# A hybrid diffusion layer on one core: retention moved beside the last recurrent pair, the output projection in one piece

## The chip, the core and the metric

The kernel runs on one core of a Trainium2 chip. The metric is the device time of one execution in microseconds (us). Five engines run their own instruction streams in order and meet at semaphores: TensorE (PE, matrix products; its weight loads are listed as PEld), VectorE (DVE), ScalarE (ACT), GpSimd (POOL), and SyncE (SP), which here issues every DMA from one queue. A profile is one execution recorded by the hardware.

## What is computed

One layer (depth 1, batch 1) over 512 latent tokens of width 2048, with 256 context tokens as a prefix. The part of the reference that the change touches:

```python
p = xm @ w_in                                         # xm: normalised, modulated latent tokens
o_rw, _ = rwkv_group(dwconv_seq(p[..., :RW_COLS], rw_conv), s_rw_c, *rw_params, readout=True)
o_ret, _ = retention_group(p[..., RW_COLS:], s_ret_c, rope=True, readout=True)
out = jnp.concatenate([o_rw, o_ret], axis=-1) @ w_out
...
x = x + g1 * rmsnorm(out, norm_post_mix[l])
h = rmsnorm(x, norm_pre_ffn[l]) * (1.0 + sc2) + sh2
y = conv_ffn(h, ffn_w_gate[l], ffn_w_up[l], ffn_conv[l], ffn_conv_b[l], ffn_w_down[l], rows)
x = x + g2 * rmsnorm(y, norm_post_ffn[l])
```

`rwkv_group` is a recurrence over 16 heads of 64 columns, `retention_group` is attention with a fixed decay over 8 heads of 128 columns. Both write 1024 of the 2048 columns that `w_out` reads. The modulation vectors (`g1`, `sh2`, `sc2`, `g2`; the kernel calls them `mod` 0 to 3) are products of one vector with a 2048 x 2048 matrix each.

## The kernel before

The code names instructions for each engine in Python; a scheduler then orders them by data, free buffers and the order in which they were named, and fixes one order per engine ahead of time. An engine that waits holds up everything behind it in its order, and so does the DMA queue on SP.

**Dense products.** Each weight block is fetched (`raw`), split into a high and a low part (`whi` on ACT, `wlo` on DVE), and each of the 16 slices of 128 rows takes three products of 128x128 by 128x512 on PE. The input projection of one 128-column tile has 16 such slices (L541 to L543).

**The recurrence.** Heads go in eight pairs. For a pair there are a preparation, a triangular solve (30 serial steps on DVE, L1182 and L1183, then small products on PE, L1197 and L1206) and a chain of eight steps (`rw_chain`: L1263, L1270, L1277, L1237, L1291 on PE with copies on ACT, sums on DVE, and one copy per direction on POOL), after which `rw_out` (PE lines L428, L441, L1335 to L1338) stores the pair's 128 rows into `o_mix` in HBM (L1340). Period p runs the chain of pair p and the preparation and solve of pair p+1, with a list `TILES` saying how many projection tiles are named among them. `behind` lets a solve's first product stand behind the projection products named so far.

**Modulation.** `ada_rest` computes one `mod` vector with 64 DVE steps of 128x512 (L846, L848) on blocks `adaw` that come by DMA, and four groups of tiny PE products (L852). `mod` 1 is spread over the periods, one step per 20 units of projection (`ADA`).

**Retention.** After the last pair, `ret_phase` fetches `o_mix` back (tile `om`), splits it into `hh` and `hl`, and runs the eight heads in two streams (even and odd heads, the second two units later), with the first half of the output projection (`out_steps`, 128 slices, L730 to L732) and all of `mod` 0 merged in by weight. A head (`retention`) loads v (`rv`), q and k (`rx`), their rotated halves (`rxs`, four DMAs each), decay tables (`dec`, `gam`), the state (`rst`) and the gate (`rg`); it turns v on PE (L767), rotates q and k (DVE L773 and L776, POOL L775), scales q twice on POOL (`qd`, L782), forms four score blocks (PE L787) that DVE multiplies by the decay (`prob`, L789), sums them (PE L800) and adds the state's part (PE L804), normalises on ACT and DVE (L808 to L812), turns the result back (PE L816) and gates it (`ro`, DVE L818). `mix_out` then runs the second half of the output projection, adds the halves and takes the norms; the ConvGLU part follows.

## Time and profile before

| | |
|---|---|
| median of 3 runs | 3353.15 us (3351.7 to 3360.01) |
| profiled execution | 3356.21 us, of which the span from first to last instruction is 3354.3 us |
| PE busy | 3168.1 us, 94% of the span |
| DVE busy | 2081.7 us, 62% |
| ACT busy | 1120.0 us, 33% |
| POOL busy | 237.5 us, 7% |
| mean granted PE clock | 0.968 of full speed |

The shares are means over stages that differ. Below, a stretch is named by its time from the span's start; a granted clock of 1.0 is 2.4 GHz and 0.5 is 1.2 GHz. "Idle before" is time in which an engine stood still just ahead of an instruction, with the instruction or transfer that ended it.

### The profile page before, as it was taken

How to read it: one execution, taken by the hardware profiler on the slowest of the kernel's cores; microseconds unless marked ns; L12 is line 12 of the kernel's file. 1: busy time of each engine (PE TensorE's matmuls, PEld its weight loads, DVE VectorE, ACT ScalarE, POOL GpSimd, SP SyncE). 2: the span in 40 equal slices, each digit the busy share in tenths (PEclk: the TensorE clock that was granted, in tenths of full speed). 3: DMA queues.
4: the chain of work that ended last, by engine and by line, in shares of the span. 5: the costliest groups of instructions: out<-in, count | busy, mean ns of one | idle time of the engine just before them, and what ended most of it. 6: DMA issues, size and time to landing. Idle time of an engine off the chain costs nothing.

```text
span 3354.3 us, 50276 instructions
## 1 busy us (share of the span) xinstructions
PE 3168.1 (94%) x19672; PEld 2507.3 (75%) x19672; DVE 2081.7 (62%) x3562; ACT 1120.0 (33%) x1954; POOL 237.5 (7%) x381
## 2 busy tenths in 40 slices
PE   5999999999999999997999899999999999999997
PEld 3688888766666776765777688888888888788885
DVE  4474767787877877765677856335643555345544
ACT  3333245434344344432232433223222222223322
POOL 0000011001111111111210100000000000000001
PEclk9999999999999999997999899999999999999998
DMA  8732222542243422426768433332423333333242
GB/s 286 272 104 77 78 84 91 157 122 89 92 148 100 150 89 88 128 69 217 232 227 280 152 110 127 110 102 94 145 90 99 101 97 104 119 104 98 95 143 102
DMA packets 197724, 433.64 MB, mean 129 GB/s; under 512 B 25360, under 2 KB 49680, under 8 KB 197488
## 3 DMA queue, kind: packets, MB, share of 16 engines
q1 hardware_dynamic: 197488, 430.45, 39.9%
q8 instruction: 154, 2.52, 0.3%
q14 instruction: 82, 0.67, 0.1%
HBM read 399.75 MB, written 30.61 MB: 128 GB/s over the span
## 4 chain that ended last, share of the span: by engine, by line
PE 47%; issue 3%; DMA 3%; DVE 2%; POOL 1%; ACT 0%; SPq 0%; POOLq 0%; DVEq 0%; ACTq 0%
PE gbank L179 14%; PE gbank L181 14%; PE gbank L180 14%; DMA adaw<-ada 2%; DVE adacc L848 1%; PE bank L787 0%; POOL y L909 0%; PE obank L732 0%; PE obank L731 0%; PE obank L730 0%; DVE wlo L204 0%; PE gbank L897 0%; PE bank L852 0%; PE gbank L898 0%; PE gbank L899 0%
## 5 line engine op out<-in xcount | busy, mean ns | idle before, releaser
L161 DVE TENSOR_TENSOR wlo<-raw,whi 128x1024 fp32r<-128x1024 f32 (+1 forms) x336 | 342.3, 1019 | 618.1 <-ACT whi L160 609.2
L160 ACT CAST whi<-raw 128x1024 fp32r<-128x1024 f32 (+1 forms) x336 | 297.1, 888 | 898.9 <-PE gbank L180 869.5
L179 PE MATMUL gbank<-hh,whi 128*128 128x512 f32 x1376 | 535.6, 389 | 0.0
L181 PE MATMUL gbank<-hh,wlo 128*128 128x512 f32 x1376 | 535.4, 389 | 0.0
L180 PE MATMUL gbank<-hl,whi 128*128 128x512 f32 x1376 | 535.4, 389 | 0.0
L203 ACT CAST whi<-raw 128x512 fp32r<-128x512 f32 (+2 forms) x320 | 211.0, 660 | 512.6 <-PE gbank L542 241.3
L543 PE MATMUL gbank<-xh,wlo 128*128 128x512 f32 (+1 forms) x896 | 367.8, 411 | 6.2 <-DVE wlo L204 6.1
L542 PE MATMUL gbank<-xl,whi 128*128 128x512 f32 (+1 forms) x896 | 368.9, 412 | 0.0
L541 PE MATMUL gbank<-xh,whi 128*128 128x512 f32 (+1 forms) x896 | 368.2, 411 | 0.2
L204 DVE TENSOR_TENSOR wlo<-raw,whi 128x512 fp32r<-128x512 f32 (+2 forms) x320 | 237.5, 745 | 102.4 <-ACT whi L203 97.5
L181 PEld LDWEIGHTS gbank<-hh,wlo 128*128 128x128 f32 x1376 | 258.3, 188 | 53.8
L180 PEld LDWEIGHTS gbank<-hl,whi 128*128 128x128 f32 x1376 | 258.3, 188 | 53.5
L179 PEld LDWEIGHTS gbank<-hh,whi 128*128 128x128 f32 x1376 | 258.3, 188 | 53.5
L181 PE MATMUL gbank<-dh,wlo 128*128 128x512 f32 x704 | 278.1, 395 | 0.2
L179 PE MATMUL gbank<-dh,whi 128*128 128x512 f32 x704 | 278.1, 395 | 0.0
L180 PE MATMUL gbank<-dl,whi 128*128 128x512 f32 x704 | 277.8, 395 | 0.0
L938 DVE SCALAR_TENSOR_TENSOR cacc<-grid,fprm,cacc 128x512 f32<-128x512 f32 x352 | 264.2, 751 | 9.9 <-ACT cacc L935 1.3
L848 DVE SCALAR_TENSOR_TENSOR adacc<-adaw,sc,adacc 128x512 f32<-128x512 f32 x240 | 187.0, 779 | 79.3 <-DMA adaw<-ada 78.0
L543 PEld LDWEIGHTS gbank<-xh,wlo 128*128 128x128 f32 (+1 forms) x896 | 170.2, 190 | 49.8 <-DVE wlo L204 8.8
L541 PEld LDWEIGHTS gbank<-xh,whi 128*128 128x128 f32 (+1 forms) x896 | 170.5, 190 | 41.4 <-issue 4.7
L542 PEld LDWEIGHTS gbank<-xl,whi 128*128 128x128 f32 (+1 forms) x896 | 170.4, 190 | 38.3 <-issue 3.1
L181 PEld LDWEIGHTS gbank<-dh,wlo 128*128 128x128 f32 x704 | 132.3, 188 | 33.4 <-DVE wlo L161 1.0
(305 smaller groups left out, 4984.1 us busy)
## 6 DMA issues: line engine op xcount, KB each, us to landing
raw<-w_in SPq DMA_DIRECT2D x284, 256.0 KB, 3.0
adaw<-ada SPq DMA_DIRECT2D x192, 256.0 KB, 3.3
raw<-w_gate SPq DMA_DIRECT2D x88, 512.0 KB, 3.7
raw<-w_up_ffn SPq DMA_DIRECT2D x88, 512.0 KB, 3.6
ada<-ada SPq DMA_DIRECT2D x64, 512.0 KB, 6.1
raw<-w_down SPq DMA_DIRECT2D x64, 512.0 KB, 3.5
raw<-w_out SPq DMA_DIRECT2D x32, 512.0 KB, 5.0
adaw<-ada SPq DMA_DIRECT2D x32, 512.0 KB, 4.5
```

What stands on the lines that cost most here:

```text
L160: nc.scalar.copy(hi[:, 0:n, 0:m], raw[:, 0:n, 0:m])
L161: nc.vector.tensor_tensor(lo[:, 0:n, 0:m], raw[:, 0:n, 0:m], hi[:, 0:n, 0:m].bitcast(F32), op=ALU.subtract)
L179: self.nc.tensor.matmul(o, hi, xh(k), start=(k == 0), stop=False)
L180: self.nc.tensor.matmul(o, hi, xl(k), start=False, stop=False)
L181: self.nc.tensor.matmul(o, lo, xh(k), start=False, stop=(k == nk - 1))
L203: nc.scalar.copy(hi[:, 0:n, 0:m], raw[:, 0:n, 0:m])
L204: nc.vector.tensor_tensor(lo[:, 0:n, 0:m], raw[:, 0:n, 0:m], hi[:, 0:n, 0:m].bitcast(F32), op=ALU.subtract)
L541: self.nc.tensor.matmul(o, hi, xh[k], start=(k == 0), stop=False)
L542: self.nc.tensor.matmul(o, hi, xl[k], start=False, stop=False)
L543: self.done = self.nc.tensor.matmul(o, lo, xh[k], start=False, stop=(k == KT - 1))
L848: nc.vector.scalar_tensor_tensor(acc, w[:, k], c, acc, op0=ALU.mult, op1=ALU.add)
L938: nc.vector.scalar_tensor_tensor(acc, grid[:, dy:dy + 8, dx:dx + 64], cw[:, f, i:i + 1], acc, op0=ALU.mult, op1=ALU.add)
```

## The change

Four things move. The list `TILES` names all 62 projection tiles within the first seven latent periods, so that none is left for the last pair. `mod` 0 follows `mod` 1 in the same periods, one step per 10 units instead of 20. The eight retention heads run in the last pair's chain: the two streams of heads and the chain with its `rw_out` are merged with equal weight and with no projection among them; the heads' pools take the place of the latent input tiles, with three instead of four buffers for `rx` and `rxs`, the decay table in a work tile, and the PSUM banks of the recurrence. A head's result is no longer split on the spot but stored into `o_mix`, now with 16 rows of tiles. The whole output projection (256 slices) then stands in `mix_out`, behind 16 loads of `om` through three buffers and their splits, with `mod` 2 spread over it at 2 and 3 steps per column tile in place of 3.

```diff
-TILES = [4, 5, 3, 5, 4, 4, 4, 5, 5, 6, 5, 5, 4]
+TILES = [4, 5, 3, 5, 4, 4, 5, 5, 6, 6, 5, 5, 5]
...
-ADAW = 3
-ADA = 20
+ADAW = 2
+ADA = 10
...
-        ada = self.ada_rest(ap, 1, 1, 2)
+        ada = chain(self.ada_rest(ap, 1, 1, 2), self.ada_rest(ap, 0, 1, 2))
...
-        for p in range(NP):
-            todo = take(len(tiles) if p == NP - 1 else TILES[nc_ + 2 + p])
-            B, steps = period(B, p)
-            fill(todo, (steps, 1.0))
+        for p in range(NP - 1):
+            work = chain(self.rw_chain(B), self.rw_out(B))
+            B = self.latent(p + 1)
+            steps = merge((work, chain_time(False), EARLY),
+                          (chain(self.rw_prep(B), self.rw_fill(B)), prep + fill_time(False), 1.0), lead=True)
+            fill(take(TILES[nc_ + 2 + p]), (steps, 1.0))
+        fill(tiles)
         pull(ada)
         esa.close()
+        esl.close()
+
+        with ExitStack() as esr:
+            self.rp = self.pool(esr, "ret", side="right", reuse_waits="tile")
+            self.rope = self.rp.tile([128, 2, L], F32, name="rope")
+            self.nc.sync.dma_start(self.rope, self.a["rope"])
+            heads = [self.retention(h) for h in range(NH)]
+            drain(merge((chain(self.rw_chain(B), self.rw_out(B)), chain_time(False), 1.0),
+                        (chain.from_iterable(heads[0::2]), 44, 1.0), (chain([LAG], chain.from_iterable(heads[1::2])), 44 + LAG, 1.0)))
...
-    def ret_phase(self):
-
...
-        drain(back())
-        heads = [self.retention(h) for h in range(NH)]
-        ada = self.ada_rest(self.rp, 0, 1, 2)
-        drain(merge((chain.from_iterable(heads[0::2]), 44, 1.0), (chain([LAG], chain.from_iterable(heads[1::2])), 44 + LAG, 1.0),
-                    (out(), OUT[0] + OUT[1], 1.0), (ada, KT // 4 * KT, ADAR)))
...
-            x = ld(i, "rx", 4)
-            xs = tile("rxs", bufs=4)
+            x = ld(i, "rx", 3)
+            xs = tile("rxs", bufs=3)
...
-            t = tile("rtmp", bufs=1)
-            nc.gpsimd.tensor_tensor(t, xs, self.rope[:, 1], op=ALU.mult)
-            nc.vector.tensor_tensor(y, y, t, op=ALU.add)
+            nc.gpsimd.tensor_tensor(xs, xs, self.rope[:, 1], op=ALU.mult)
+            nc.vector.tensor_tensor(y, y, xs, op=ALU.add)
...
-        self.split(o, self.hh[NP + h], self.hl[NP + h])
+        nc.sync.dma_start(self.o_mix[NP + h], o)
...
     def mix_out(self):
         nc, a, mp = self.nc, self.a, self.mp
+        order = [*range(NP, KT), *range(NP)]
+        ys = [self.yp.tile([128, L], F32, name=f"y{c}") for c in range(KT)]
+        for k in order:
+            t = mp.tile([128, L], F32, name="om", bufs=3)
+            nc.sync.dma_start(t, self.o_mix[k])
+            self.split(t, self.hh[k], self.hl[k])
+        wst = self.stream([a["w_out"][c, :, k:k + 8] for c in range(KT) for k in (NP, 0)])
         acc = mp.tile([128, L], F32, name="acc")
-        ys = self.ys
         ada = self.ada_rest(mp, 2)
         for c in range(KT):
             ps = self.gbank()
-            drain(self.out_steps(ps, 1))
-            nc.vector.tensor_tensor(ys[c], ps, ys[c], op=ALU.add)
-            sq = self.square(mp, ys[c])
+            for k in order:
+                hi, lo = next(wst)
+                nc.tensor.matmul(ps, hi, self.hh[k], start=(k == NP), stop=False)
+                nc.tensor.matmul(ps, hi, self.hl[k], start=False, stop=False)
+                nc.tensor.matmul(ps, lo, self.hh[k], start=False, stop=(k == NP - 1))
+            sq = self.square(mp, ps)
+            nc.scalar.copy(ys[c], ps)
...
-            pull(ada, ADAW)
+            pull(ada, ADAW + c % 2)
```

What this makes of the engines' orders shows at three places. The line numbers of the changed program differ from those above, and the names say which operation it is.

**SP, the loads of the third and fourth head.** Before, they stand among the blocks of `mod` 0 (`adaw`):

```order
L743 DMA rv<-ret_t 128x512
L832 DMA adaw<-ada 128x512
L743 DMA rx<-ret_t 128x512
L755 DMA rxs<-ret_t 32x512
L832 DMA adaw<-ada 128x512
L755 DMA rxs<-ret_t 32x512
L832 DMA adaw<-ada 128x512
L755 DMA rxs<-ret_t 32x512 x2
L832 DMA adaw<-ada 128x512
L743 DMA rx<-ret_t 128x512
```

In the changed order (here from the third head's state `rst` on), the stores of the first two heads (`o_mix<-ro`) stand among the fourth head's loads, and its last three rotated quarters come behind the second store:

```order
L721 DMA rst<-ret_s 128x256
L704 DMA rv<-ret_t 128x512
L704 DMA rx<-ret_t 128x512
L714 DMA rxs<-ret_t 32x512 x3
L777 DMA o_mix<-ro 128x512
L704 DMA rg<-ret_t 128x512
L714 DMA rxs<-ret_t 32x512
L704 DMA rx<-ret_t 128x512
L714 DMA rxs<-ret_t 32x512
L777 DMA o_mix<-ro 128x512
L714 DMA rxs<-ret_t 32x512 x3
```

The blocks of `mod` 0 have left this queue, and each pair of heads has put two stores into it.

**PE, one pair of heads.** Before, the scores (L787) and the sums (L800, L804) of a pair stand behind a run of output projection (L730 to L732), of which the last three products are shown:

```order
L730 MATMUL obank<-hh_16378,whi 128x512
L731 MATMUL obank<-hl_16394,whi 128x512
L732 MATMUL obank<-hh_16378,wlo 128x512
L787 MATMUL bank<-rot 128x512 x4
L800 MATMUL gbank<-rvt,prob 128x128 x4
L787 MATMUL bank<-rot 128x512
L800 MATMUL gbank<-rvt,prob 128x128 x8
L787 MATMUL bank<-rot 128x512
L800 MATMUL gbank<-rvt,prob 128x128 x4
L804 MATMUL gbank<-rst,qd 128x128 x8
L800 MATMUL gbank<-rvt,prob 128x128 x8
L804 MATMUL gbank<-rst,qd 128x128 x8
```

In the changed order the same pair's scores (L745) and sums (L758, L762) follow the last chain step's products (L1245, L1205) directly:

```order
L1245 MATMUL bank<-w,tt 64x64 x4
L1205 MATMUL obank<-rt_15358,sv 64x64
L1205 MATMUL obank<-rt_15536,sv 64x64 x2
L745 MATMUL bank<-rot 128x512 x4
L758 MATMUL gbank<-rvt,prob 128x128 x4
L745 MATMUL bank<-rot 128x512
L758 MATMUL gbank<-rvt,prob 128x128 x8
L745 MATMUL bank<-rot 128x512
L758 MATMUL gbank<-rvt,prob 128x128 x4
L762 MATMUL gbank<-rst,qd 128x128 x8
L758 MATMUL gbank<-rvt,prob 128x128 x8
L762 MATMUL gbank<-rst,qd 128x128 x8
```

The output projection is gone from between the pairs, and nothing but the chain of the last pair took its place.

**SP, the way into the output projection.** In the changed order all `om` loads stand behind the stores of the last pair (`o_mix<-t`) and of the last head, and the first `w_out` block behind three of them:

```order
L777 DMA o_mix<-ro 128x512
L1308 DMA o_mix<-t_17273 128x512
L777 DMA o_mix<-ro 128x512
L826 DMA om<-o_mix 128x512 x3
L192 DMA raw<-w_out 128x1024
L826 DMA om<-o_mix 128x512 x3
L192 DMA raw<-w_out 128x1024
L790 DMA adaw<-ada 128x1024
```

Before, the eight `om` loads stood among the first head's loads and the first `w_out` blocks behind these:

```order
L709 DMA om<-o_mix 128x512 x2
L758 DMA dec<-rtab 128x896
L760 DMA gam<-rgam 128x512
L762 DMA rst<-ret_s 128x256
L709 DMA om<-o_mix 128x512 x2
L743 DMA rg<-ret_t 128x512
L195 DMA raw<-w_out 128x1024 x2
L832 DMA adaw<-ada 128x512 x2
```

So one transition from stores to loads to products moved behind the heads, and it carries 16 tiles now instead of eight.

## Rows read from the trace of the kernel before

**Rows 1.** The page: its head line, and a row of its DMA issues.

```profile
span 3354.3 us, 50276 instructions
...
raw<-w_out SPq DMA_DIRECT2D x32, 512.0 KB, 5.0
```

**Rows 2.** Windows: length, then PE, PEld, DVE, ACT, POOL busy (instructions), PEclk, DMA, GB/s.

```profile
1170.20:1269.30 99.10, 95.16 (x807) 69.60 (x807) 77.60 (x166) 40.94 (x81) 12.39 (x25) 0.94 0.29 93
1269.30:1380.20 110.90, 106.64 (x862) 79.05 (x862) 88.86 (x187) 44.50 (x86) 14.16 (x25) 0.95 0.41 130
...
1479.80:1546.50 66.70, 45.20 (x532) 31.33 (x532) 22.57 (x45) 22.83 (x50) 9.95 (x16) 0.80 0.35 114
1546.50:1740.00 193.50, 178.89 (x923) 141.34 (x924) 124.76 (x168) 53.99 (x152) 40.99 (x28) 0.96 0.72 233
```

**Rows 3.** Windows of L541 alone (one product per slice of projection).

```profile
1479.80:1546.00 66.20, 7.82 (x18) 3.37 (x18) 0.80 0.35 114
```

**Rows 4.** Windows of L848 alone (modulation steps on DVE), seven latent periods.

```profile
1269.30:1380.20 110.90, 11.22 (x15) 0.95 0.41 130
...
sum 725.20, DVE 33.73; mean DVE 4.82
```

**Rows 5.** Timeline of PE: two solves (start, us, instruction, idle before and releaser).

```profile
1170.25 0.26 PE L1197 MATMUL bank<-t,nt 32*32 32x32 f32 x1 [4.42 <-DVE t L1188]
...
1479.82 0.21 PE L1197 MATMUL bank<-t,nt 32*32 32x32 f32 x1 [2.15 <-DVE t L1188]
```

**Rows 6.** Timeline of PE: the last pair's chain, then the first head's scores.

```profile
1483.82 0.45 PE L1263 MATMUL bank<-sv,xa 128*64 128x64 f32 x8
...
1510.89 0.45 PE L1263 MATMUL bank<-sv,xa 128*64 128x64 f32 x8 [0.72 <-DVE sv L1301]
...
1514.73 0.45 PE L1263 MATMUL bank<-sv,xa 128*64 128x64 f32 x8 [1.38 <-DVE sv L1301]
...
1537.10 3.61 PE L787 MATMUL bank<-rot 128*128 128x512 f32 x4 [10.12 <-DVE rot L776]
```

**Rows 7.** Timeline of SP (DMA issues) around the last pair's store.

```profile
1515.96 0.90 SPq L755 DMA_DIRECT2D rxs<-ret_t  x2
1526.85 0.34 SPq L1340 DMA_DIRECT2D o_mix<-t  x1
1527.23 0.90 SPq L755 DMA_DIRECT2D rxs<-ret_t  x2
```

**Rows 8.** Timeline of PE: sums and scores of a pair, back to back.

```profile
1572.41 1.05 PE L800 MATMUL gbank<-rvt,prob 128*128 128x128 f32 x8
1573.30 1.02 PE L787 MATMUL bank<-rot 128*128 128x512 f32 x2
1574.16 1.95 PE L800 MATMUL gbank<-rvt,prob 128*128 128x128 f32 x16
```

**Rows 9.** Groups by line, 1546.5 to 1740 (busy us, mean ns; idle before, releasers).

```profile
L775 POOL TENSOR_TENSOR rtmp<-rxs,rope 128x512 f32<-128x512 f32 x14 | 20.5, 1461 | 77.7 <-DMA rxs<-ret_t 69.6 <-DVE adacc L848 6.3 <-DVE rot L776 1.6
...
L812 ACT ACTIVATE ry<-gbank,rss 128x128 f32<-128x128 f32 x32 | 9.1, 368 | 7.0 <-DVE rss L810 7.0
L808 ACT ACTIVATE ry<-gbank 128x128 f32<-128x128 f32 x32 | 8.4, 285 | 44.6 <-PE gbank L804 44.6
```

**Rows 10.** Timeline of PE: the second head's state products in the first and last pair.

```profile
1585.20 1.95 PE L804 MATMUL gbank<-rst,qd 128*128 128x128 f32 x16
...
1731.97 1.16 PE L804 MATMUL gbank<-rst,qd 128*128 128x128 f32 x8 [0.40 <-POOL qd L782]
```

**Rows 11.** Timeline of PE: the last products of the output projection.

```profile
1837.60 0.39 PE L731 MATMUL gbank<-hl,whi 128*128 128x512 f32 x1
1837.83 0.39 PE L732 MATMUL gbank<-hh,wlo 128*128 128x512 f32 x1
```

**Rows 12.** Instructions on the tile `om` (durations ns min/median/max), and its loads.

```profile
L223 ACT CAST hh<-om x8: 617/618/621, 1527.5 to 1543.4; 128x512 fp32r<-128x512 f32 x8
L224 DVE TENSOR_TENSOR hl<-om,hh x8: 684/692/1473, 1528.2 to 1544.0; 128x512 fp32r<-128x512 f32 x8
...
DMA to landing us min/median/max: 2.6/3.5/4.2
```

**Rows 13.** Windows, columns as in Rows 2: the end of the chain and the first head.

```profile
1516.50:1540.40 23.90, 11.07 (x52) 7.15 (x52) 10.56 (x18) 7.37 (x13) 3.05 (x2) 0.50 0.55 180
```

More of the change, by code (lines that the diff above doesn't have):

```diff
@@ L47 @@
 NW = 3
-OUT = [0.0, 1.0]
-ADAR = 0.9
-ADAW = 3
-ADA = 20
+ADAW = 2
+ADA = 10
 EV = 4
@@ L239, in run @@
                 self.wp = self.pool(esw, "weights", side="right", reuse_waits="tile")
-                self.xp = self.pool(esw, "x_lat", side="right", reuse_waits="tile")
+                esl = ExitStack()
+                self.xp = self.pool(esl, "x_lat", side="right", reuse_waits="tile")
                 self.xc = self.pool(esx, "x_ctx", side="right", reuse_waits="tile")
@@ L266, in run @@
                 self.hl = [self.fp.tile([128, L], F32R, name=f"hl{k}") for k in range(KT)]
-                self.wst = self.stream([self.a["w_out"][c, :, k:k + 8] for k in (0, 8) for c in range(KT)])
-                with ExitStack() as es2:
-                    self.ps_g = self.pool(es2, "ps_g3", bufs=3, space=PSUM, reuse_waits="tile")
-                    self.ps_rw = self.pool(es2, "ps_r3", bufs=3, space=PSUM, reuse_waits="tile")
-                    self.ps_out = self.pool(es2, "ps_o3", bufs=2, space=PSUM, reuse_waits="tile")
-                    self.rp = self.pool(es2, "ret", side="right", reuse_waits="tile")
-                    self.ret_phase()
                 self.ps_g = self.pool(es1, "ps_g2", bufs=5, space=PSUM, reuse_waits="tile")
@@ L331, in mixers @@
         fill(take(TILES[nc_ + 1]), (chain(self.rw_prep(B), self.rw_fill(B)), 1 / (prep + fill_time(False))))
-        def period(B, p):
-            streams = [(chain(self.rw_chain(B), self.rw_out(B)), chain_time(False), EARLY)]
-            if p + 1 < NP:
-                B = self.latent(p + 1)
-                streams.append((chain(self.rw_prep(B), self.rw_fill(B)), prep + fill_time(False), 1.0))
-            return B, merge(*streams, lead=True)
-        for p in range(NP):
-            todo = take(len(tiles) if p == NP - 1 else TILES[nc_ + 2 + p])
-            B, steps = period(B, p)
-            fill(todo, (steps, 1.0))
+        for p in range(NP - 1):
[5 more added lines that the diff above has]
+        fill(tiles)
         pull(ada)
         esa.close()
+        esl.close()
[6 more added lines that the diff above has]
+                        (chain.from_iterable(heads[0::2]), 44, 1.0), (chain([LAG], chain.from_iterable(heads[1::2])), 44 + LAG, 1.0)))
         esw.close()
@@ L378, in setup @@
         self.sg = self.dr.tile([2, 128, L], F32, name="sg0"), self.dr.tile([96, L], F32, name="sg1")
-        self.o_mix = self.dr.tile([NP, 128, L], F32, name="o_mix")
+        self.o_mix = self.dr.tile([KT, 128, L], F32, name="o_mix")
     def rw_setup(self):
@@ L698, in ret_context @@
         nc.sync.dma_start(self.ret_s[h].rearrange("p d e -> p (d e)"), s)
-    def ret_phase(self):
-        nc = self.nc
-        self.rope = self.rp.tile([128, 2, L], F32, name="rope")
-        self.ys = [self.yp.tile([128, L], F32, name=f"y{c}") for c in range(KT)]
-        def back():
-            for k in range(NP):
-                t = self.rp.tile([128, L], F32, name="om", bufs=NOM)
-                nc.sync.dma_start(t, self.o_mix[k])
-                self.split(t, self.hh[k], self.hl[k])
-                yield 1
-        def out():
-            yield OUT[0]
-            for c in range(KT):
-                ps = self.obank()
-                yield from self.out_steps(ps, 0)
-                nc.scalar.copy(self.ys[c], ps)
-        drain(back())
-        heads = [self.retention(h) for h in range(NH)]
-        ada = self.ada_rest(self.rp, 0, 1, 2)
-        drain(merge((chain.from_iterable(heads[0::2]), 44, 1.0), (chain([LAG], chain.from_iterable(heads[1::2])), 44 + LAG, 1.0),
-                    (out(), OUT[0] + OUT[1], 1.0), (ada, KT // 4 * KT, ADAR)))
-    def out_steps(self, ps, half):
-        for k in range(8 * half, 8 * half + 8):
-            hi, lo = next(self.wst)
-            self.nc.tensor.matmul(ps, hi, self.hh[k], start=(k % 8 == 0), stop=False)
-            self.nc.tensor.matmul(ps, hi, self.hl[k], start=False, stop=False)
-            self.nc.tensor.matmul(ps, lo, self.hh[k], start=False, stop=(k % 8 == 7))
-            yield OUT[1] / (8 * KT)
     def retention(self, h):
@@ L756, in retention @@
             raw.append((x, xs))
-        dec = tile("dec", 896)
+        dec = self.t4()[:, 0:896]
         nc.sync.dma_start(dec, a["rtab"][h])
@@ L764, in retention @@
         yield 1
-        pv = self.gbank()
+        pv = self.bank()
         for c in range(4):
@@ L813, in retention @@
         yield 3
-        po = self.gbank()
+        po = self.bank()
         for n in range(4):
```

11 lines of the change are left out of this document (4 added, 7 removed).

## The prediction

> **What bounds the kernel now.** I read the page first, then windows by stage, then the waits and timelines inside the stages that the change touches. The windows show PE busy for 95.2 of 99.1 us in an ordinary latent period and 178.9 of 193.5 us in the stretch with retention, which also carries half the output projection and all of `mod` 0 [rows 2]. So PE's work sets the time, and a change can win only what PE idles or does at the low clock. The worst place is between the last solve and the output projection: 45.2 busy of 66.7 us, clock 0.80 [rows 2].
>
> The timelines say why. With the projections used up, a step of the last chain takes 1514.73 - 1510.89 = 3.84 us [rows 6]. Then PE stands 10.1 us for the first head's rotated q and k [rows 6]: on SP the loads of the rotated quarters stop behind the store of the last pair's result, which waits for its data from 1516.86 to 1526.85, and go on at 1527.23 [rows 7]. A store on this queue holds up every load named after it. Later the heads wait too, on POOL for `rxs` (69.6 us) [rows 9], but the output projection fills PE meanwhile.
>
> I compare the stretch from the last solve's first product (1479.8) [rows 5] to the last product of the output projection (1838.1: 1837.83 and one spacing more) [rows 11], which is 358.3 us. What lies before and after it does the same work in both kernels, but for the periods, which I treat first.
>
> **Part A, the seven periods.** Only 18 slices of projection still run after the last solve's start [rows 3], though three tiles (48) are named there: the scheduler had already pulled the others forward. Thus 18 x 3 = 54 products move ahead of the solve, at 0.23 us each, the spacing of dense products [rows 11]: 12.4 us. They fill gaps there today, and will be plain additional time in front. `mod` 0 brings its tiny PE products too, four groups, an estimated 1 us each: 4 us, which it saves later.
>
> `mod` 0 also brings 60 more large DVE steps into these periods: each of the seven gets 15, and today they hold 33.73 / 0.75 = 45 [rows 4]. At 0.75 us (11.22 over 15) [rows 4] that is 45 us of DVE work. The cover is idle DVE time: 77.6 busy of 99.1 us, and 88.9 of 110.9 with 15 steps in it [rows 2]. The cover is not perfect, because PE ends each period waiting for DVE's solve: 2.15 us in the last period, which has no such steps, and 4.42 us in a period with 15 [rows 5]. If the steps are hidden the cost is 0; if all are serial it is 45 us. The rows nearest to the case are the two waits, which differ by 2.3 us; three of the seven periods hold such steps already, so I take 1 us for each, 7 us in all. Part A: 12.4 + 4 + 7 = 23 us, bounds 16 and 61.
>
> **Part B, the chain with the heads, from the solve's start to the last head's product.**
> - Solve to chain: 1483.82 - 1479.82 = 4.0 us [rows 5, 6].
> - The order puts five of the eight chain steps ahead of the bulk of the first pair of heads. Little stands among them, so they go at the bare step: 5 x 3.84 = 19 us [rows 6]; two scores and two sums among them cost about 2 us more. The first head's loads are named behind the last projection's store and have landed by then.
> - A head costs PE four scores at 0.86 us, four sums at 0.89 [rows 8], 1.95 for the state [rows 10] and about 0.6 of turns (estimate): 9.5 us. The rest of the first pair is 19 - 4.3 = 14.7 us.
> - Three further pairs at 19 us of PE work, 57 us. Each has a wait at its head. POOL needs 2 x 1.46 us to turn one head's q and k [rows 9], and the second head's last quarters stand on SP behind the stores of the pair before. Such a store leaves only when ACT has squared and scaled that head's sums (4 x 0.285 and 4 x 0.368 [rows 9], one head after the other) and the result is turned and gated: an estimated 10 us after the state's products. The loads land about 3 us later, POOL and DVE add 2 to 3 us: some 17 us after the mark, of which PE can fill 12. I take 5 us of idle for each pair, 15 us, and 8 us for three chain steps and `rw_out`: 80 us.
> - The last pair's normalisation, turn and gate are bare: 8 us.
> - The clock. Where PE worked 11.1 of 23.9 us the granted clock was 0.50 [rows 13], 1.2 of 2.4 GHz. The five bare steps and each pair's head look like that, and work done then takes twice as long: I charge 12 us.
>
> Together 4 + 21 + 14.7 + 80 + 8 + 12 = 140 us. The lower bound has every pair's wait filled and a full clock, 140 - 15 - 12 = 113. The upper one takes the pairs at today's cycle with the projection in it, (1731.97 - 1585.20) / 3 = 48.9 us [rows 10] in place of 27: 140 + 3 x 22 = 206.
>
> Today's cycle gives a second reading of the three pairs: 48.9 us less 32 slices x 3 x 0.23 = 22 us of projection is 27 us for a pair, 81 us for three, if nothing of the projection lay under a wait. The Trainium skill speaks against this part ("Perfetto Trace Analysis", section Optimization Strategy): where the engine that limits changes over time, interleaving such regimes may help. Here regimes that were interleaved are taken apart, and by that rule the projection did lie under waits, so that a pair would keep up to its whole 48.9 us, which is the upper bound. If the projection hid nothing, the pairs would fall to their bare 57 us.
>
> **Part C, the output projection in one piece.** After the last head's product come its store, the first `om` loads, and fifth in the queue the first `w_out` block. The block lands 5.0 us after its issue [rows 1]; with 0.45 us for each issue (0.90 for two [rows 7]) and its cast, an estimated 1 us, the first product comes 8 us after the last head is gated. Then 16 `om` tiles go through three buffers. One takes 3.5 us to land, 0.62 on ACT, 0.69 on DVE [rows 12] and some 0.4 to be issued: 5.2 us, so 16 / 3 x 5.2 = 28 us until all are split. Meanwhile the order lets PE do about 24 of the 256 slices (16 us); some of the 28 us lies under the first 8, and I charge 9 us. All 768 products at the dense spacing are 768 x 0.2275 = 175 us [rows 11], and the waits for `mod` 2's sums cost some 7 us. Part C: 8 + 9 + 175 + 7 = 199 us, bounds 185 and 212. The additions of the two halves and the copies fall away on DVE and ACT, which are not what is waited for: 0.
>
> **The sum.** 23 + 140 + 199 = 362 us against 358.3: 4 us more. Against the profiled execution that is 3356.2 + 4 = 3360; the median of the runs stands 3 us below the profiled one, so I say 3357 us. The change buys back the 10 us stall and the second transition, and pays with bare chain steps, bare head waits and a longer transition of its own.
>
> **The rivals.** A difference below 0.3%, 10 us, is about what a measurement of this kernel can't tell from no change.
> - *No change that can be told* (the forecast), 3346 to 3364: chance 0.38.
> - *Faster: the stores do not hold the loads.* If the loads run a pair ahead, the three waits (15 us), most of the clock charge and DVE's 7 us vanish: 4 - 15 - 9 - 7 = -27 against today, 3326. For it: three buffers hold a head and a half. Against it: a store did just this in [rows 7]. It decides where the waits of the pairs, the clock and DVE together cost 14 us less than I charge. Chance 0.25.
> - *Slower: the cycle of a pair is the loads' and POOL's, not PE's.* Today POOL waits for `rxs` and the cycle is 48.9 us with only 41 us of PE work in it. If a pair takes 36 us instead of 27, the time is 3357 + 27 = 3384; from 31 us on it is slower by more than 10. Chance 0.23.
> - *Slower: the clock stays low through part B.* The Trainium skill ("TensorE: Matmul & The Clock Gate", section Why this matters for your kernels) wants no idle gaps between bursts of products. In rows: part B holds 8 x 9.5 = 76 us of heads and an estimated 25 us of solve, chain and `rw_out`; if half of that runs at 0.50 as in [rows 13], it costs 50 us in place of the 12 charged: 3395. Against it: with retention's products in it the long stretch kept a mean of 0.96 [rows 2]. Chance 0.07.
> - *Slower: DVE sets the periods.* With all 45 us of `mod` 0 serial the time is 3357 + 38 = 3395. Against it stands DVE's idle time [rows 2]. Chance 0.07.
>
> **The numbers.** Faster 0.25, same 0.38, slower 0.37. The range goes from the faster rival, 3326, to just short of the last two, 3391; for the forecast alone it is 3346 to 3364.
>
> **What would show it.** Right: 54 products fewer behind the last solve's start, which comes near 1503; a wait of PE for DVE's solve of 2 to 5 us in each period; chain steps of about 4 us with low clock behind it; state products of successive pairs 25 to 30 us apart; o_mix stores on SP with rotated quarters right behind them; first output product about 8 us after the last gate, then 768 at 0.23 us. Wrong: pairs 20 us apart (faster) or over 31 (slower), solve waits of 7 us or more, or a clock of 0.5 through the heads.

## The result and the profile after the change

The changed kernel takes 3389.48 us (median of 4 runs, 3384.61 to 3393.52) against 3355.69 us (3351.70 to 3360.01) for the kernel before: a ratio of 1.010, 95% interval 1.0078 to 1.0122. It is 1% slower. That lies near the upper end of the range; the forecast proper, no change that can be told, did not come true. The profiled execution took 3386.5 us. Two executions of kernels further below, 4881.75 and 4392.80 us long at a mean granted clock of 0.58 and 0.65, are left out of every ratio.

The page of the changed kernel: its head line, the busy time of the engines, and the row on the blocks of `w_out`, which answers to [rows 1].

```profile
span 3384.7 us, 50268 instructions
...
PE 3186.3 (94%) x19672; PEld 2520.9 (74%) x19672; DVE 2063.0 (61%) x3546; ACT 1118.8 (33%) x1954; POOL 231.1 (7%) x381
...
raw<-w_out SPq DMA_DIRECT2D x32, 512.0 KB, 4.6
```

The span grew by 30.4 us with about as many instructions. Windows show the stage. The row by itself is the seven latent periods of the kernel before. Of the three behind it, of the changed kernel, the first is the same periods, the second runs from the last solve's first product to the first output product, the third is the output projection. The columns are those of [rows 2].

```profile
754.60:1479.80 725.20, 689.47 (x5792) 505.17 (x5792) 582.61 (x1226) 293.96 (x576) 90.16 (x174) 0.96 0.35 110
```

```profile
752.70:1524.60 771.90, 717.21 (x5888) 527.89 (x5888) 621.85 (x1299) 297.42 (x580) 90.71 (x175) 0.94 0.42 128
1524.60:1679.50 154.90, 121.60 (x972) 92.21 (x972) 67.11 (x111) 40.82 (x151) 46.36 (x44) 0.80 0.48 151
1679.50:1869.70 190.20, 184.84 (x804) 148.41 (x805) 104.42 (x130) 57.12 (x76) 1.29 (x1) 0.98 0.67 221
```

The periods cost 771.9 - 725.2 = 46.7 us more. The stretch behind them, 358.3 us before, is 345 us: 13 us less. So the loss is in front of the part that was rebuilt. Two windows of single periods, and the modulation steps alone in one of them and in all seven, answer to [rows 2] and [rows 4]:

```profile
1307.50:1415.80 108.30, 100.05 (x840) 73.46 (x842) 88.28 (x185) 41.14 (x83) 13.05 (x25) 0.95 0.43 131
1415.80:1524.60 108.80, 97.83 (x826) 71.71 (x826) 86.51 (x184) 41.44 (x80) 13.46 (x25) 0.92 0.37 114
```

```profile
1415.80:1524.60 108.80, 11.28 (x15) 0.92 0.37 114
...
sum 771.90, DVE 79.00; mean DVE 11.29
```

The last period does 97.8 us of PE work, a little more than the 95.2 us of the ordinary period of before, and takes 108.8 us in place of 99.1. What PE waits for in the seven periods (us in total, times, longest), in the changed kernel and then in two rows of the kernel before:

```profile
PE bank L1165 <- DVE t L1156: 20.6, 8, 4.8
PE gbank L539 <- DVE wlo L201: 12.9, 6, 3.7
PE bank L1231 <- DVE t L1150: 7.3, 5, 3.5
PE bank L1116 <- DVE t L1091: 5.6, 4, 2.8
PE bank L1231 <- DVE sv L1269: 4.9, 4, 2.6
```

```profile
PE bank L1197 <- DVE t L1188: 19.7, 8, 4.4
...
PE gbank L543 <- DVE wlo L204: 3.8, 5, 1.1
```

The first row is the wait for the solve, which the prediction watched. It is 19.7 us in the kernel before: it did not grow. What grew are the others: for the low part of the split weights (`wlo`, 12.9 us for 3.8), and those of the chain's products for VectorE while it is in the solve (L1150) or still at the chain's sums (L1269). All of these wait for VectorE's work, late.

The waits are not the whole loss. Window less busy time, PE stands idle for 54.7 us in the seven periods where it stood for 35.7 before: 19.0 us more. Its busy time grew by 27.7 us. The 54 moved products are 12.4 of that, and most of the rest goes with the granted clock, 0.94 over the periods for 0.96: 689.5 us of work at 0.96 would take some 704 at 0.94 (an estimate from the two rows).

### The profile page after: what moved, and what is told of

It is laid out like the page before. It is cut to its first block, busy times and chain, and to the rows that moved or that the text cites. A ratio compares the mean times of both kernels' runs of the same rounds, so it can differ in the third digit from the quotient of the medians.

```text
span 3384.7 us, 50268 instructions
## 1 busy us (share of the span) xinstructions
PE 3186.3 (94%) x19672; PEld 2520.9 (74%) x19672; DVE 2063.0 (61%) x3546; ACT 1118.8 (33%) x1954; POOL 231.1 (7%) x381
## 3 DMA queue, kind: packets, MB, share of 16 engines
q1 hardware_dynamic: 199792, 434.64, 40.8%
## 4 chain that ended last, share of the span: by engine, by line
PE 46%; DMA 2%; DVE 2%; POOL 0%; ACT 0%; issue 0%; SPq 0%; POOLq 0%; ACTq 0%; DVEq 0%
PE gbank L178 14%; PE gbank L176 14%; PE gbank L177 14%; DMA adaw<-ada 1%; PE gbank L835 1%; PE gbank L837 1%; PE gbank L836 1%; DVE adacc L806 1%; DMA om<-o_mix 0%; DVE wlo L201 0%; POOL y L877 0%; PE gbank L865 0%; PE gbank L866 0%; PE bank L745 0%; PE gbank L867 0%
```

## The experiments

Each ratio is to the kernel before, run on the same chip. Before the latent periods identical code ends anywhere from 749.6 to 761.5 us into a profile, so stages are compared by their own windows, and whole times by their ratios. A window shows one execution. Five of the kernels below have the same periods, without vector 0, and these take 721.2, 728.1, 734.7, 734.8 and 737.3 us. PE is idle for 34.6 to 35.8 us in all five; what differs is its busy time, and the granted clock with it. The shortest and the longest:

```profile
757.80:1479.00 721.20, 685.62 (x5831) 503.82 (x5831) 585.91 (x1228) 296.29 (x579) 88.85 (x174) 0.97 0.36 111
```

```profile
752.30:1489.60 737.30, 701.55 (x5834) 514.55 (x5836) 586.15 (x1228) 296.80 (x579) 88.64 (x174) 0.95 0.35 108
```

So the length of the periods in one profile is good to some 16 us, and PE's idle time in them to about 1 us.

**Without vector 0, and vector 0 beside the heads.** The first kernel leaves vector 0 out, with a constant in its place, and asks what it costs in the periods; the second does all the work.

```diff
-ADA = 10
+ADA = 20
-        ada = chain(self.ada_rest(ap, 1, 1, 2), self.ada_rest(ap, 0, 1, 2))
+        ada = self.ada_rest(ap, 1, 1, 2)
...
 # e1_no_mod0, behind the periods:
+        self.nc.vector.memset(self.mod[:, 0], 0.1)
 # e2_mod0_ret, in the merge of the last chain with the heads:
+            ada = self.ada_rest(self.rp, 0, 1, 2)
+                        (ada, KT // 4 * KT, 0.9)))
```

> This kernel leaves out modulation vector 0 (a constant stands in its place) and is otherwise the changed one, with five to fifteen column steps in a period as before the change. Theory M (the 64 column sums of vector 0 on VectorE make the splits, transposes and sums that the products wait for late, and the clock falls behind those waits): the seven latent periods shrink from 771.9 us to about 740 (725.2 of before and some 14 for 18 more products' slices of 0.23 us times 3), and the kernel from 3389 to about 3356. Rival S (the periods are longer because of how the projections are spread over them, 5 to 6 a period for 4 to 5, and the column sums are hidden): the periods stay at 762 or more, the kernel at 3378 or more, less only the 4 us of TensorE sums and a few us.

> The whole computation; the 64 column sums of vector 0 are taken from the seven periods and merged, one behind another, into the stretch of the last chain and the heads. Theory M: periods about 740 us as without vector 0; in the stretch of the heads VectorE goes from 67 to about 115 us of work in 155, which costs 0 to 20 us there, so the kernel comes to 3356 to 3376. Rival S: periods 762 or more and the kernel at 3385 to 3400, since the sums only add to the heads' stretch. If VectorE is what paces the heads (a rotation and a reciprocal stand in line on it), the stretch from the last solve to the first output product grows from 155 to 175 us or more.

Without vector 0: ratio 0.9995 (0.998 to 1.001). The periods take 734.8 us. Counting one product per slice of projection in them gives these windows, of this kernel and of the changed one:

```profile
756.20:1491.00 734.80, 236.03 (x561) 0.95 0.35 109
```

```profile
752.70:1524.60 771.90, 238.19 (x564) 0.94 0.42 128
```

Three slices more are 2 us, so vector 0 costs 37 - 2 = 35 us there; against the other profiles of these periods it is 33 to 49. Of the 35, 20 are idle time of PE (54.7 us for 34.7). Theory M holds. With vector 0 beside the heads the ratio is 1.0154 (1.0132 to 1.0177), slower still, and beyond what either theory gave for the whole. Its periods are as short (734.7 us), but from the last solve to the first output product it takes 222 us instead of 161.7. The expectation names such a growth last, with VectorE as the pace of the heads, and this is more than its size. That VectorE is the pace is not shown: it works 114.2 of the 222 us, and GpSimd waits 77.2 us for the rotated quarters (`rxs`), whose loads share SyncE's queue with vector 0's. PE's two largest waits in that stretch:

```profile
PE bank L747 <- DVE rot L736: 34.7, 4, 13.5
PE bank L812 <- DVE adacc L808: 18.3, 3, 9.2
```

The first is the heads' rotation, late; the second is TensorE's own sum over a finished block of vector 0, which stands in PE's order and waits for VectorE's column sums.

**One part of the change alone.** Into the kernel before, only vector 0's move:

```diff
-ADA = 20
+ADA = 10
-        ada = self.ada_rest(ap, 1, 1, 2)
+        ada = chain(self.ada_rest(ap, 1, 1, 2), self.ada_rest(ap, 0, 1, 2))
...
-        ada = self.ada_rest(self.rp, 0, 1, 2)
-                    (out(), OUT[0] + OUT[1], 1.0), (ada, KT // 4 * KT, ADAR)))
+                    (out(), OUT[0] + OUT[1], 1.0)))
```

> The kernel before the change with one part of it alone: vector 0's 64 column sums move from beside the heads into the seven latent periods, the projections and the heads stay where they were. Theory M: the periods grow from 725.2 to about 755 us, the stretch of the heads gains a few us back (VectorE has less in it), so the kernel goes from 3356 to 3376 to 3386. Rival S: the periods grow by 8 us or less and the kernel stays within 3350 to 3362.

Measured: 0.9989 (0.9974 to 1.0003), no change. The expectation failed on its second half. The windows are the periods, the stretch from the last solve to the last output product, the last period, and one pair of heads; the row behind them is PE's main wait in the last period.

```profile
761.50:1526.40 764.90, 706.05 (x5882) 519.43 (x5882) 620.52 (x1297) 299.55 (x582) 95.29 (x175) 0.95 0.41 131
1526.40:1849.00 322.60, 298.69 (x1785) 240.85 (x1788) 170.51 (x255) 96.60 (x226) 48.57 (x45) 0.91 0.57 183
...
1419.80:1526.40 106.60, 82.51 (x758) 58.89 (x758) 84.09 (x177) 37.01 (x74) 12.94 (x25) 0.87 0.37 115
...
1659.40:1700.20 40.80, 40.80 (x223) 32.82 (x222) 18.09 (x26) 12.04 (x37) 10.27 (x8) 1.00 0.41 129
```

```profile
PE bank L1196 <- DVE t L1187: 23.8, 2, 21.2
```

The move lengthens the periods by 39.7 us, more than M's 30, and gives the heads' stretch 358.3 - 322.6 = 35.7 us back, not a few. Both numbers hold a second move: the scheduler drew the last 18 slices of projection into the periods here too (564 for 546), an estimated 12.4 us of products on either side. This profile is also of the slowest of the kernel's ten runs, 11.6 us above their median. The last period shows a floor under a period: only 82.5 us of PE work is left in it, PE stands 21.2 us for the solve, and it still takes 106.6 us. And with vector 0 gone from beside them, a pair of heads with its share of the projection keeps PE busy for 40.80 of 40.80 us, at a clock of 1.00.

**Where in a period a column sum stands.** In the changed kernel and in the one just shown, the sums of both vectors are held back until the running solve's last transposition has been issued; the work of the whole kernel is the same.

```diff
-                        pull(ada, (gone + t) // ADA - gone // ADA)
+                        self.owe += (gone + t) // ADA - gone // ADA
+                        if self.owe and not self.solving:
+                            pull(ada, 1)
+                            self.owe -= 1
...
+                            self.tc.add_manual_dep(add.ins, self.solved.ins.name,
+                                                   mybir.DependencyInfo(mybir.DependencyClass.NoSync, mybir.DependencyReason.DATA), reason="order")
```

> The changed kernel with the same work on the same engines, but the column sums of both vectors held back on VectorE until the running solve's last transposition, so that none stands inside a solve (before, 9 to 15 stood in each). Theory S (the sums cost what they are long, because they stand in the solve's line on VectorE and the products of a period can't cover a longer solve): the solves take 31 to 35 us for 39 to 46, the periods 735 to 750 for 772, and the kernel 3352 to 3368. Rival W (VectorE's whole work of some 95 us in a period counts, wherever a sum stands; the sums then delay the splits, the preparation and the chain): the solves shrink, the periods stay at 762 or more, and the kernel at 3380 or more.

> The kernel before the change with vector 0 moved from the heads' stretch into the seven periods, the column sums of both vectors held back behind each solve in the same way. With the sums in the solves this move cost the periods 40 us and gave the heads' stretch 36 back. Theory S: periods 725 to 740, the heads' stretch keeps its 36, the kernel at 3318 to 3335, faster than both. Rival W: periods 755 or more, the kernel at 3350 or more.

The changed kernel so edited: 1.0052 (1.0034 to 1.0071) in place of 1.010, half of the loss. Its last solve and its last three periods, then the last solve of the changed kernel (the columns of [rows 2]):

```profile
1460.70:1492.70 32.00, 31.80 (x245) 23.94 (x246) 29.41 (x82) 11.18 (x24) 3.96 (x8) 1.00 0.37 112
...
1187.70:1292.90 105.20, 98.91 (x844) 72.63 (x843) 90.30 (x185) 43.22 (x84) 11.82 (x25) 0.97 0.43 134
1292.90:1396.60 103.70, 97.01 (x841) 70.85 (x841) 90.36 (x185) 41.28 (x83) 11.33 (x25) 0.98 0.44 137
1396.60:1498.00 101.40, 95.74 (x839) 69.82 (x838) 90.05 (x185) 40.83 (x82) 10.88 (x23) 1.00 0.39 122
```

```profile
1481.40:1520.50 39.10, 38.18 (x276) 29.59 (x276) 34.28 (x93) 12.89 (x25) 4.52 (x8) 0.96 0.49 156
```

The solve is 7 us shorter, and periods with 80 or 81 slices and 15 sums take 101 to 105 us where the changed kernel's last three, with 73 to 80 slices, take 108 to 111. All seven take 754.5 us with 572 slices, where 561 and no vector 0 took 734.8. With 0.69 us for a slice (three products at 0.23) the rest is 19.7 - 7.6 = 12 us, so that 23 of the 35 would be due to the place inside the solve. These windows can't carry that number: PE's idle time in the periods fell only from 54.7 to 49.0 us, and the remainder is busy time, which moves by 16 us between profiles of equal periods. The ratio says half. Theory S is right in direction for this kernel and too large in size. The new waits say where the rest sits:

```profile
PE bank L1239 <- DVE sv L1277: 15.6, 9, 5.6
PE bank L1253 <- ACT w L1241: 12.5, 6, 3.7
```

PE now waits in the chain, for its sums on VectorE and for the ACT copies between. Besides, the stretch behind the periods grew from 154.9 to 167.1 us. Sums that were held back run there now, 11 of them with 8.84 us of VectorE's time, where the changed kernel has none (this kernel's periods and the stretch behind them, VectorE's sums alone):

```profile
743.50:1498.00 754.50, 80.05 (x108) 0.95 0.42 131
1498.00:1665.10 167.10, 8.84 (x11) 0.79 0.56 168
```

So the edit did not only move sums within a period: the periods hold 108 sums for 105, some held back from ahead of them, and lose 11 at their end. Four slices of projection moved behind the last solve too. The run without vector 0 has 161.7 us there, with three such slices and no sums.

The kernel of before with the same edit is at 0.9994 (0.998 to 1.0009), where it was at 0.9989 without. Its periods take 760.3 us for 764.9 and hold 537 slices for 564, since the order of the projections moved with the sums, and one of them is 125 us long; 19 of its sums run behind the last solve, and the stretch from there to the last output product takes 337.2 us for 322.6. By the whole time that is rival W's. Why the gain of the first kernel does not appear here stays open.

**Another engine.** Vector 0 at its places in the periods, on GpSimd:

```diff
-                        nc.vector.scalar_tensor_tensor(acc, w[:, k], c, acc, op0=ALU.mult, op1=ALU.add)
+                        nc.gpsimd.tensor_scalar(w[:, k], w[:, k], c, None, op0=ALU.mult)
+                        nc.gpsimd.tensor_tensor(acc, w[:, k], acc, op=ALU.add)
```

> The changed kernel, vector 0's loads and steps at their places in the seven periods, but each column sum done by GpSimd (one product with the column's scale, one addition, an estimated 1.46 us each from the tensor operations of the heads) and not by VectorE: VectorE loses 45 us of work there, GpSimd gains some 185 us. Theory M (VectorE's path through the solve sets the period where it holds 15 steps): the periods shrink from 772 to 735 to 745 us and the kernel from 3389 to 3355 to 3365. Rival T (what costs is the traffic of the weights, the places on SyncE's queue, or TensorE's sums): the periods stay at 765 or more. A mishap that would speak for neither: GpSimd's own small copies of the solve and the preparation now wait behind its sums, up to 3 us each, which would show as waits for GpSimd.

> The kernel before the change, with vector 0 moved from the heads' stretch into the seven periods, and its column sums done by GpSimd there. On VectorE the same move cost the periods 40 us and gave the heads' stretch 36 back. Theory M: the periods stay at 725 to 735 us, the heads' stretch keeps its 36 us, and the kernel is at 3320 to 3330, faster than both. Rival T: the periods grow to 755 or more and the kernel is at 3350 to 3360.

Both got slower: 1.0141 (1.011 to 1.0172) and 1.0112 (1.0074 to 1.015), with periods of 788.3 and 800.0 us. Vector 1 comes first in these kernels, so GpSimd works on vector 0 only from the end of the third period on. In the last three periods of the first kernel the solves take 39, 39 and 32 us (40, 40 and 39 in the changed kernel), the first two as long as with sums in them, and the periods 119.9, 117.9 and 112.6. The largest wait of PE in its seven periods is one that the expectation named as a mishap:

```profile
PE bank L1234 <- POOL sv L1197: 30.7, 7, 8.2
```

```profile
L806 POOL TENSOR_SCALAR adaw<-adaw,sc 128x512 f32<-128x512 f32 x60 | 108.1, 1802 | 37.1 <-DMA adaw<-ada 35.6
L807 POOL TENSOR_TENSOR adacc<-adaw,adacc 128x512 f32<-128x512 f32 x60 | 81.8, 1364 | 5.0
```

GpSimd's small copies of the chain (`sv`) stand behind its column sums, and PE behind the copies. The second kernel shows a further cost, which the expectations did not have: VectorE's own operations got longer. The first operations of the solve's 30 steps take 10.15 us in its third period, where GpSimd does one product of a sum, and 18.98 us in the fourth, where it does 14:

```profile
974.80:1084.70 109.90, 10.15 (x30) 0.95 0.42 134
1084.70:1201.70 117.00, 18.98 (x30) 0.89 0.36 110
```

One of these steps, which takes 0.29 us in the changed kernel, takes 1.39 us beside an addition on GpSimd that ends 0.15 us before it:

```profile
1388.59 1.41 POOL L848 TENSOR_TENSOR adacc<-adaw,adacc 128x512 f32<-128x512 f32 x1
```

```profile
1388.76 1.39 DVE L1184 TENSOR_TENSOR t<-t 128x130 f32<-128x130 f32 x1
```

VectorE is busy for 650.2 us in this kernel's seven periods, for 582.6 in the kernel before, with 1228 and 1226 instructions. In the first kernel the same steps are that slow in one period alone (15.28 us in the fourth, 10.6 at most in the others). So these two runs tell neither for M nor for T: the sums left VectorE, but what took their place delayed it, the chain and PE.

**Vector 0 beside the output products.**

```diff
-        ada = self.ada_rest(mp, 2)
+        ada = chain(self.ada_rest(mp, 0), self.ada_rest(mp, 2))
...
-            pull(ada, ADAW + c % 2)
+            pull(ada, 4 + c % 2)
```

> The whole computation; vector 0's 64 column sums are taken from the seven periods and done beside the dense output products, ahead of vector 2's. Theory M (a column sum costs what it delays, and the dense part has DVE idle for 86 of 190 us): the periods come back to about 735 us as in the run without vector 0, the output part stays within 188 to 195 us with VectorE at some 150 us of work in it, and the kernel is at 3350 to 3360, even with the kernel before. Rival D (VectorE, or the loads of two vectors beside those of the output weights, then set the output part): the output part grows to 205 us or more and the kernel stays above 3370.

> The kernel before the change with vector 0's column sums taken from the heads' stretch and done beside the second half of the output projection, with vector 2's. Moving them into the periods gave the heads' stretch some 36 us back and cost the periods 40. If the second half (some 90 us, with 128 column sums of 0.75 us, 96 us of VectorE work) becomes VectorE's, it grows by 20 to 35 us and the kernel is at 3340 to 3356; if VectorE keeps up, the kernel is at 3318 to 3330.

The changed kernel so edited: 1.004 (1.0025 to 1.0055). Its output part takes 206.5 us for 190.2:

```profile
1640.70:1847.20 206.50, 194.03 (x836) 155.41 (x840) 150.18 (x199) 57.19 (x76) 0.89 (x1) 0.96 0.84 284
```

DMA moves 284 GB/s here for 221 in the changed kernel, and VectorE's sums wait 26.8 us for their weights. The periods do come back, to 721.2 us in this profile, the fastest of the kernel's ten runs, but the output part gives 16 us of that away again, as rival D has it. In the kernel before, with five steps for each column tile in place of three, there are half the products to hide under, and vector 2 already brings DMA to 286 GB/s and VectorE to 76 of 91 us. That is worse, 1.0139 (1.0113 to 1.0164): PE waits 60.5 us for the column sums when the projection is over. Both terms of that expectation were too hopeful.

**More buffers, and the stores from another queue.** The second kernel with vector 0 beside the heads, with five weight buffers for two; then the heads' stores issued by ScalarE, in the changed kernel and in the one with vector 0 beside the output products.

```diff
-            ada = self.ada_rest(self.rp, 0, 1, 2)
+            ada = self.ada_rest(self.rp, 0, 1, 5)
...
-        nc.sync.dma_start(self.o_mix[NP + h], o)
+        nc.scalar.dma_start(self.o_mix[NP + h], o)
```

> The kernel with vector 0 merged into the heads' stretch, which took 222 us from the last solve to the first output product for 155, now with five buffers for the weights of vector 0 where it had two. Theory L (a load of these weights stands on SyncE's queue until VectorE has freed its buffer, and the heads' loads stand behind it): SyncE runs four steps ahead instead of one, and the stretch falls to 185 to 205 us, the kernel from 3414 to 3380 to 3397. Rival V (the 48 us of VectorE work in the stretch set its length): it stays at 215 us or more and the kernel above 3405.

> The changed kernel with the heads' result stores issued from ScalarE's queue and not from SyncE's, where the next heads' rotated quarters stand behind them. Theory Q (the store holds the loads: the quarters of the second head of a pair are issued only when the head before is stored): the cycle of a pair goes from 31 us to about 26, the stretch from the last solve to the first output product from 155 to about 143, the kernel from 3389 to about 3377. Rival B (the loads wait for their buffers, which GpSimd and VectorE give back, or ScalarE is held by the store in its turn): the cycle stays at 30 to 32 and the kernel at 3386 to 3392, or above it.

> As the kernel with vector 0 beside the dense output products, and the heads' result stores issued from ScalarE's queue as well. If the two repairs add up, it takes 7 us off that kernel, 3343 to 3353: the stretch from the last solve to the first output product is 147 to 155 us and the periods 735. If the gain of the stores was the spread of one profile, both kernels are alike within 3 us.

Five buffers: 1.0142 (1.0122 to 1.0162), the stretch 213.5 us for 222. Between the two theories, nearer to V by its numbers: the buffers account for some 8 us of the 60. That VectorE's work sets the length is still not shown; it works 115.4 of the 213.5 us. PE's wait for the rotation falls from 34.7 to 10.5 us, and one of 23.8 us for the load of `rv` takes its place.

The stores: 1.0078 (1.0057 to 1.0099), not to be told from 1.010; with vector 0 beside the output products, 1.0025 (1.001 to 1.004) after 1.004, which is alike within 3 us. In the changed kernel with moved stores the stretch from the last solve to the first output product is 146.7 us for 154.9. The state products that end a pair start at 1574.59, 1604.58, 1633.64 and 1661.06: 30.0, 29.1 and 27.4 us apart, some 5 us less in all than in the changed kernel (31.8, 31.2 and 28.6). With vector 0 beside the output products the same edit takes this stretch only from 161.7 to 160.5 us, so the 8 us did not come a second time. SyncE's waits in this stretch of the kernel with the moved stores say why theory Q's 26 us did not come:

```profile
SPq L721 <- PE gbank L762: 14.0, 3, 5.4
SPq L717 <- DVE prob L747: 12.5, 3, 9.5
SPq L704 <- DVE ro L776: 10.8, 4, 4.8
SPq L714 <- DVE rot L734: 9.1, 2, 6.2
```

In the changed kernel the store itself is the first of these, 35.5 us in 8 waits. With it gone the loads behind it stand for their own buffers: `rst`, the decay table, `rg`, `rxs`. This is rival B's reason, though the cycle fell a little below its 30 to 32 us.

No kernel here beats the one of before by more than can be measured.

## Why the prediction was right or wrong

**Part A failed at the price of vector 0's steps.** The count of the moved products was right: 564 slices in the seven periods, and 564 - 18 = 546 before, are 54 products, 12.4 us. The run without vector 0, with 15 slices more than before, takes 9.6 us more, which fits but is less than such windows differ by themselves. Wrong was "I take 1 us for each, 7 us in all" for vector 0's steps, with 4 us for its TensorE sums: 11 us, where the runs show 35 (33 to 49 by profile). 20 of them are idle time of PE, and the others are busy time, in part at a lower clock, for which Part A has no term. With the 12.4 that makes 47 for the 46.7 measured, from the same windows.

The price was read from PE's wait for the solve, 2.15 us without steps and 4.42 with them [rows 5]. That wait was a poor gauge. PE's products stand in a fixed order, and it comes to the solve late because it has already waited for splits, transposes and chain sums: in the changed kernel the solve waits are the same and the last period is some 10 us longer than the ordinary one of before. The better gauge stood in [rows 2]: 99.1 us without steps and 110.9 with them. I read that difference as PE work (95.2 and 106.6 us), and there it is: those periods hold 72 and 88 slices. But it also shows how the kernel before hid its steps. It had them in periods where the products covered a longer solve. The same 15 steps in periods of 73 to 80 slices are not covered, and the period stays near 108 us; with 52 slices it stays at 106.6. This is how it looks if a period is the longer of two paths, PE's products and VectorE's solve with the steps in it. The run that takes the sums out of the solve bears it out for about half of the cost; in the kernel before the same edit gained nothing, so how much is the place in the solve and how much VectorE's work as a whole stays open. Either way the runs speak for the rival "DVE sets the periods", which had a chance of 0.07, and its serial 45 us was nearer than 7. That the time lies inside the range all the same is luck: the range ended just short of this rival's 3395 us, and not at a bound of the term that failed.

**Part B was 7 us short.** It took 147 us for 140, from 1524.63 to the last gate at 1671.8. To the end of the first pair 50.3 us passed (39.7 predicted, the clock's 12 aside), three further pairs took 91.8 (80), the tail 5.1 (8). The pairs, 31.8, 31.2 and 28.6 us apart, show the mechanism as it was described: the order on SyncE, with the loads right behind the store, then the second head's scores.

```profile
1610.25 0.34 SPq L777 DMA_DIRECT2D o_mix<-ro  x1
...
1614.20 0.33 SPq L777 DMA_DIRECT2D o_mix<-ro  x1
1614.59 1.36 SPq L714 DMA_DIRECT2D rxs<-ret_t  x3
```

```profile
1606.70:1638.20 31.50, 26.37 (x139) 19.20 (x139) 14.00 (x23) 7.73 (x33) 11.12 (x9) 0.78 0.64 197
```

But the cause was half told. The queue's order is not what sets the cycle alone: without the store in it the pairs gain 1 to 2 us each, and the same loads then wait for their buffers. The granted clock in such a pair was 0.78; it did not stay at 0.50 through the heads. The rival "the cycle of a pair is the loads' and POOL's" named 31 us as its threshold and has its 12 us in the total.

**Part C was right in its sum.** The first output product starts at 1679.52, 7.7 us after the last gate (8 predicted), and the projection takes 190 us (191).

```profile
1679.52 0.80 PE L835 MATMUL gbank<-hh,whi 128*128 128x512 f32 x1 [9.03 <-ACT whi L200]
...
1869.35 0.39 PE L837 MATMUL gbank<-hh,wlo 128*128 128x512 f32 x1
```

Its terms were less right, and partly cancel: PE is idle for 5.4 of the 190.2 us, where 16 were charged for waits, and busy for 184.8, where the products had 175.

The sum: 46.7 for 23, 147 for 140, 198 for 199, which is 391.7 us against the 358.3 of before, 33 us more, and 3 us less elsewhere.

**What the sum hid.** Set against the kernel with vector 0's move alone, the change reads otherwise. That move is neutral: 39.7 us lost in the periods, 35.7 won behind them. Counted in this order, the rest of the change, retention under the chain and the projection apart, is what costs the 1%: from 764.9 and 322.6 us to 771.9 and 345. In [rows 10] a pair took 48.9 us, and the prediction held that only 41 of them were PE work. The trace of the kernel before says otherwise: over these three pairs PE is busy for 137.24 of 146.8 us, 45.7 a pair, with 102 slices of projection in them and vector 0's TensorE sums.

```profile
1585.20:1634.10 48.90, 45.93 (x257) 37.16 (x256) 33.99 (x46) 15.86 (x51) 10.26 (x7) 1.00 0.75 237
1634.10:1683.00 48.90, 46.22 (x231) 37.03 (x230) 30.24 (x42) 9.90 (x21) 10.09 (x8) 0.93 0.69 228
1683.00:1732.00 49.00, 45.09 (x242) 35.26 (x240) 34.88 (x45) 15.40 (x41) 12.11 (x9) 1.00 0.72 230
```

Only 3 us of such a pair were idle. Without vector 0 the pair is 40.80 us of pure PE work, about 19 for the heads and some 21 for the projection (91 slices in three pairs, at 0.69 us), with nothing idle at full clock. Pulled apart, the heads alone take 29 to 32 us a pair and the 21 us are paid again later: 9 to 12 us more for a pair. The Trainium skill ("Perfetto Trace Analysis", section Optimization Strategy) holds that interleaving may help where the limiting engine changes over time. The trace agrees, 40.8 us together against 29 to 32 and some 21 apart, though the upper bound of 48.9 that the prediction drew from it was not reached.

## What to carry to other kernels

A step that fits into an engine's idle time by the sum can still cost most of its length: compare stages with and without it that hold the same other work, by all of the idle time of the engine that sets the pace and by its clock, and not by the one wait that the step is expected to lengthen. Before work is taken from beside other work, look at how busy the limiting engine is in the joint stretch: here a pair of heads with its projection left PE idle for 3 of 49 us, and without vector 0 for none, so that little was to be won by taking it apart. When a store moves off a queue, check what the loads behind it wait for next.

## What was not expected of the hardware

A column sum that is one operation of 0.75 us on VectorE takes two on GpSimd, 1.80 us for the product with a column and 1.36 us for the addition, where 1.46 us each was expected. Beside such sums, VectorE's steps of the solve took 18.98 us in a period where they take 10.15 without. And the output part, with two vectors' weights beside `w_out`, took 206.5 us at 284 GB/s, with 150 us of work for VectorE and 194 for PE in it.
